# A sliding-window attention stage with its scores moved to the head of the turn

## The chip, the cores and the metric

One core of one Trainium2 chip runs the whole program. The metric is device time in microseconds (us); the kernel before takes 1373.77 us, the median of 3 runs (1372.44 to 1374.89). TensorE is PE in the profile (its weight loads are PEld), VectorE is DVE, ScalarE is ACT, GpSimd is POOL and SyncE is SP.

## The reference

A trunk of two layers on x (1024 tokens, width 1024, float32). Layer 0 normalises x, projects it once into six parts and runs two mixers side by side: a recurrent one (RG-LRU) and the sliding-window attention, whose stage the change rewrites. Layer 1 is a gated MLP with chunked spatial mixing; the change does not touch it. Cut to what matters:

```
z = rms_norm(x) @ w_in_a            # columns: za, ga (recurrent) | zq, zk, zv, gb (attention)
q = rms_norm(zq per head); k = rms_norm(zk per head)     # 16 query heads, 2 key/value heads, width 64
for each block of 128 queries:      # keys: the block before and the block itself, 256
    sc  = q @ k.T / 8 + bias[head]  # relative-position bias, -inf outside the window of 128
    m   = max(max(sc), sink[head])
    p   = exp(sc - m);  denom = sum(p) + exp(sink - m)
    out = (p / denom) @ v
y = concat(ya * silu(ga), yb * silu(gb));  x = x + y @ w_out_a
```

## The kernel before

**Precision.** Products run on pairs of float32r tiles, a high part and the rest (`hi` and `lo`, `h` and `l`), so one product is three matmuls (`mm3`, L144). Weights are split so by `load_weights` (L127): ScalarE casts the high part (L133), VectorE takes the rest (L134).

**Units.** The attention stage has 32 units: 4 groups `c` of 4 heads, times 8 blocks `b` of 128 tokens (`units`). A unit goes through these helpers:

- `att_bias` (L512): bias tile times the query's rms into `e`, two heads by GpSimd (L524) and two by ScalarE (L521). `e` has three buffers.
- `att_s` (L528): eight score matmuls into two PSUM banks, and per head one VectorE operation that scales, adds the bias and takes the maximum (L549); then `nm` (L554) and `es` (L557).
- `att_exp` (L560): exponentials on ScalarE, one for `es` and four for the heads, with sums.
- `att_scale` (L568): the two key blocks' probabilities are added (L573; because values are given as `v_more`, the difference of neighbouring blocks, one 128-wide product and a masked one do the work), then denominators, reciprocal and scaling.
- `att_pt` (L581): four transposes on TensorE, `ph` by ScalarE (L588), `pl` by VectorE (L589), and GpSimd's two masked copies `mh` and `ml` (L595).
- `att_pv` (L599): up to four matmuls into `pv`; ScalarE copies two halves to `ot` (L609, L610).
- `att_out` (L613): VectorE adds the other halves (L616, L617), GpSimd multiplies into `yb` (L619).

**The loop.** Turn t of the loop at L655 works on several units at once: scale of unit t-2, transposes and `pv` of t-3, bias and scores of t, exponentials of t-1. Between them TensorE gets filler work in halves of a projection, each 12 large matmuls: `q_step` makes the queries of the head group half a group ahead (two halves and then `q_parts`, which squares and splits the queries, and `q_stats`, eight small matmuls `st`, `qm` on VectorE, `pow` on GpSimd), `gb_step` the gate of the next group, and from group 3 on `mix_a_first` and `mix_a_part` the recurrent mixer's first products (`za`, `ga`). At the first unit of a group `gb_silu` (L360) takes ScalarE to the SiLU table over a 128x2048 tile.

**What sets the order.** `manual_schedule` keeps TensorE everywhere, and ScalarE, VectorE and GpSimd in this stage, in the order in which the code issues their instructions. In a turn of the kernel before VectorE's order is scale, `pl`, weight split, query remainders, `qm`, score operations, `es`, `out`; ScalarE's is `ph`, bias, exponentials, SiLU, weight cast, queries, evacuation of `gb`, `ot` copies; GpSimd's is masks, bias, `pow`, `yb`. PE's is transposes, `q_step`, `gb_step`, `pv`, statistics, scores. SP (the DMA queue) is ordered by the planner. `SPLIT_STEPS` says at which block b which weights are split; five weight tiles are held. The planner may also place work of the next stage (splits of the recurrent mixer's weights) into the end of this one. Eight PSUM banks are shared by all accumulators.

Of the kernel before, what the change touches and what calls it, by code (L numbers as in the profile page):

```python
# [14 lines left out]
ALU = mybir.AluOpType  # L15
# [3 lines left out]
P = 128  # L19
# [9 lines left out]
SPLIT_STEPS = {2: 7, 3: 8, 4: 9, 6: 10}  # L29
# [32 lines left out]
def trunk_kernel(  # L62
# [4 lines left out]
    nc = tc.nc  # L67
# [3 lines left out]
    x, out = x[0], out[0]  # L71
# [8 lines left out]
    def bank(name):  # L80
        return ps.tile([P, 512], F32, tag="p", name=name)

    def big_tile(dt, name):
        return big.tile([P, 2048], dt, tag="m", name=name)
# [42 lines left out]
    def load_weights(i, prefetch=True):  # L127

        for j in range(len(wtiles), min(i, last_spec[0]) + 1):
            fetch_weights(j)  # L130
            hi = wpool.tile(list(raws[j].shape), F32R, tag="wh", name=f"wh{j}")
            lo = wpool.tile(list(raws[j].shape), F32R, tag="wl", name=f"wl{j}")
            nc.scalar.copy(out=hi, in_=raws[j])  # L133
            nc.vector.tensor_tensor(out=lo, in0=raws[j], in1=hi.bitcast(F32), op=ALU.subtract)  # L134
            wtiles.append((hi, lo))
            if prefetch:
                fetch_weights(j + 2)
# [211 lines left out]
    def gb_step(c, f, half, khalf):  # L349

        if yb[c] is None:
            yb[c] = big_tile(F32, f"yb{c}").rearrange("p (f s) -> p f s", f=2)
        if khalf == 0:
            gb_acc[0] = bank(f"gb{c}_{f}_{half}")
        acc = gb_acc[0]
        proj_stationary_w(acc, ("gb", 2 * c + f), hh, hl, half * 512, khalf * 4, khalf * 4 + 4)
        return (yb[c][:, f, half * 512:(half + 1) * 512], acc) if khalf == 1 else None

    def gb_silu(c):
        nc.scalar.activation(out=yb[c], in_=yb[c], func=AF.Silu)  # L360
# [95 lines left out]
    units = [(c, b) for c in range(4) for b in range(NT)]  # L456
    state = [dict() for _ in units]
# [13 lines left out]
    def q_step(hc, j):  # L471

        c, half = divmod(hc, 2)
        p, kh = divmod(j, 2)
        if kh == 0:
            q_state["acc"] = bank(f"pq{hc}_{p}")
        proj_stationary_w(q_state["acc"], ("q", c, p), hh, hl, half * 512, kh * 4, kh * 4 + 4)
        return kh == 1
# [20 lines left out]
    def q_stats(hc, p, sq):  # L499

        acc = bank(f"st{hc}_{p}")
        for b in range(4):
            nc.tensor.matmul(acc[:, 2 * b:2 * b + 2], lhsT=sq[:, b, :], rhs=pair_ones, start=True, stop=True)
        m = small.tile([P, 8], F32, tag="qm", name=f"qm{hc}_{p}", bufs=2)
        rs = small.tile([P, 8], F32, tag="qrs", name=f"qrs{hc}_{p}", bufs=5)
        rms = small.tile([P, 8], F32, tag="qrms", name=f"qrms{hc}_{p}", bufs=5)
        nc.vector.tensor_scalar(out=m, in0=acc[:, :8], scalar1=1.0 / HD, scalar2=EPS, op0=ALU.mult, op1=ALU.add)
        nc.gpsimd.tensor_tensor(out=rs, in0=m, in1=half_neg, op=ALU.pow)
        nc.gpsimd.tensor_tensor(out=rms, in0=m, in1=rs, op=ALU.mult)
        q_state[hc][1].append((rs, rms))  # L510

    def att_bias(u):  # L512

        c, b = units[u]
        k0 = 0 if b else P
        e = at.tile([P, 4, 256], F32, tag="e", name=f"e{u}", bufs=3)
        for hp in range(2):
            rms = q_state[2 * c + b // 4][1][hp][1]
            if hp:
                for j in range(2):  # L520
                    nc.scalar.mul(e[:, 2 + j, k0:256], bias_tile(2 * c + hp)[:, j, k0:256],  # L521
                                  rms[:, 2 * (b % 4) + j:2 * (b % 4) + j + 1])
                continue
            nc.gpsimd.tensor_tensor(out=e[:, 2 * hp:2 * hp + 2, k0:256], in0=bias_tile(2 * c + hp)[:, :, k0:256],  # L524
                                    in1=bc(rms[:, 2 * (b % 4):2 * (b % 4) + 2], 2, 256 - k0), op=ALU.mult)
        state[u]["e"], state[u]["k0"] = e, k0
# [33 lines left out]
    def att_exp(u):  # L560
        st = state[u]
        e = st["e"][:, :, st["k0"]:256]
        nc.scalar.activation(out=st["es"], in_=st["es"], func=AF.Exp)
        for h in range(4):
            nc.scalar.activation(out=e[:, h], in_=e[:, h], func=AF.Exp,  # L565
                                 bias=st["nm"][:, h:h + 1], accum_out=st["sums"][:, h:h + 1])

    def att_scale(u):  # L568
        st = state[u]
        e = st["e"]  # L570
        p = st["p"] = e[:, :, 0:P] if units[u][1] else e[:, :, P:256]
        if units[u][1]:
            nc.vector.tensor_tensor(out=p, in0=p, in1=e[:, :, P:256], op=ALU.add)  # L573
        den = small.tile([P, 4], F32, tag="den", name=f"den{u}")
        nc.vector.tensor_tensor(out=den, in0=st["sums"], in1=st["es"], op=ALU.add)
        nc.vector.reciprocal(out=den, in_=den)
        nc.vector.tensor_tensor(out=p, in0=p, in1=bc(den, 2, P), op=ALU.mult)
# [3 lines left out]
    def att_pt(u):  # L581
        st = state[u]
        pt = bank(f"ppt{u}")
        for h in range(4):
            nc.tensor.transpose(pt[:, h * P:(h + 1) * P], st["p"][:, h, :], ident)
        ptv = pt.rearrange("p (j i s) -> p i j s", j=2, i=2)
        ph, pl = [at.tile([P, 2, 2, P], F32R, tag=f"p{r}", name=f"p{r}{u}", bufs=1) for r in "hl"]
        nc.scalar.copy(out=ph, in_=ptv)  # L588
        nc.vector.tensor_tensor(out=pl, in0=ptv, in1=ph.bitcast(F32), op=ALU.subtract)  # L589
        st["parts"] = [part.rearrange("p i j s -> p (i j s)") for part in (ph, pl)]  # L590
        st["before"] = []
        if units[u][1]:
            for r, part in zip("hl", st["parts"]):
                m = at.tile([P, 512], F32R, tag=f"m{r}", name=f"m{r}{u}", bufs=1)
                nc.gpsimd.affine_select(out=m, in_=part.bitcast(F32), pattern=[[0, 4], [1, P]], compare_op=ALU.is_ge,  # L595
                                        fill=0.0, base=-P, channel_multiplier=1)
                st["before"].append(m)
# [27 lines left out]
    def mix_a_part(n, kind, half, khalf):  # L625

        if khalf == 0:
            mix_acc[n, kind, half] = bank(f"{kind}{n}_{half}")
        proj_stationary_w(mix_acc[n, kind, half], (kind, n), hh, hl, half * 512, khalf * 4, khalf * 4 + 4)
# [6 lines left out]
    def mix_a_first(b):  # L636

        if b == 0:
            za0[0] = big_tile(F32, "za0").rearrange("p (i s) -> p i s", i=2)
        i, half, kh = b // 4, (b // 2) % 2, b % 2  # L640
        mix_a_part(0, ("za", "ga")[i], half, kh)
        return (za0[0][:, i, half * 512:(half + 1) * 512], mix_acc[0, ("za", "ga")[i], half]) if kh else None

    NU = len(units)
# [4 lines left out]
    sq = q_parts(0, 0)  # L649
# [2 lines left out]
        q_step(0, j)  # L652
    q_stats(0, 0, sq)
    sq = q_parts(0, 1)
    for t in range(NU + 3):  # L655
        c, b = divmod(t, NT)
        new = t < NU
        hc, j = t // 4 + 1, t % 4
        q_done, evac = False, None
        if 2 <= t < NU + 2:  # L660
            att_scale(t - 2)
        if t >= 3:
            att_pt(t - 3)
        if new:
            if hc < 8:
                q_done = q_step(hc, j)
            else:
                mix_a_part(1, "za", j // 2, j % 2)
            if t == 0:
                q_stats(0, 1, sq)  # L670
            att_bias(t)
        if 1 <= t <= NU:
            att_exp(t - 1)
        if new and c and b == 0:
            gb_silu(c)
        if new:
            evac = gb_step(c + 1, b // 4, (b // 2) % 2, b % 2) if c < 3 else mix_a_first(b)
        else:
            for kh in range(2):
                mix_a_part(*((1, "ga", t - NU) if t < NU + 2 else (2, "za", 0)), kh)  # L680
        if new and b in SPLIT_STEPS:
            load_weights(SPLIT_STEPS[b] + 4 * c)
        sq = q_parts(hc, j // 2) if q_done else None
        if evac:
            nc.scalar.copy(out=evac[0], in_=evac[1])
        if t >= 3:
            att_pv(t - 3)
        if q_done:
            q_stats(hc, j // 2, sq)
        if new:  # L690
            att_s(t)
        if t >= 3:
            att_out(t - 3)
    manual.__exit__(None, None, None)
    p1.close()
    const_c = ctx.enter_context(tc.tile_pool(name="const_c", bufs=1))
# [227 lines left out]

    manual = tc.manual_schedule(engines={ET.Activation, ET.DVE})
    manual.__enter__()
    for kh in range(2):
        mix_a_part(2, "za", 1, kh)
    conv = mix_a_conv(0)
    split = mix_a_split(0, conv)  # L930
    ys = [mix_a_silu(0)]
# [507 lines left out]
```

## Time and profile before

| | |
|---|---|
| median of 3 runs | 1373.77 us (1372.44 to 1374.89) |
| profiled execution | 1376.04 us, span 1374.3 us, granted TensorE clock 0.994 of full speed |
| busy over the span | PE 1329.9 us (97%), PEld 1123.6 (82%), DVE 1000.4 (73%), ACT 691.9 (50%), POOL 229.7 (17%) |
| chain that ended last | PE 68%, DVE 18%, ACT 4%, DMA 4%, issue 3%, POOL 2% |
| DMA | 131.38 MB in 97170 packets, mean 96 GB/s |
| attention stage | scores from 85.9 to 366 us, last `pv` product started at 387.51 |

The busy time of an engine is summed over the profiled span; a busy TensorE includes overlapping matmuls, so what counts is the spacing of their starts. In a timeline row stand the start, the duration, the engine, the line, the operation, output<-inputs, the shape and the count; in brackets the idle time just before it and what ended it.

### The profile page before, as it was taken

To read this page: it belongs to the slowest core of one execution; us is meant where nothing else is said; L and a number is where in the kernel's file an instruction comes from. 1 tells how busy PE (TensorE), PEld (TensorE's weight loads), DVE (VectorE), ACT (ScalarE), POOL (GpSimd) and SP (SyncE) were. 2 spreads that over 40 slices of the span, in tenths; PEclk is the share of its full clock that TensorE was granted. 3 is DMA by queue.
4 is the path that set the end of the run, shared out by engine and by line. 5 is a ranking of instruction groups with operands and counts; after the bars stand their busy time and mean duration, and the time that the engine had idled before them with its cause. 6 is when DMAs were issued, how large, how long until landed. Compare 5 with 4: busy or idle time off the path is not lost.

```text
span 1374.3 us, 17785 instructions
## 1 busy us (share of the span) xinstructions
PE 1329.9 (97%) x6775; PEld 1123.6 (82%) x6775; DVE 1000.4 (73%) x1622; ACT 691.9 (50%) x1246; POOL 229.7 (17%) x212
## 2 busy tenths in 40 slices
PE   7999999999889999989999899999999999999998
PEld 6987877777767888878888899888888888888887
DVE  6568787888767878996987655566666556669974
ACT  5466767676558778433554332344344444343331
POOL 2344545544413323000000000000000000000000
PEclk9999999999999999999999999999999999999999
DMA  6111111111211102511423332413332333497131
GB/s 220 38 42 46 31 46 32 47 31 47 62 43 39 50 23 108 210 65 62 153 108 100 100 108 93 139 62 107 108 109 69 107 109 114 141 376 255 50 113 62
DMA packets 97170, 131.38 MB, mean 96 GB/s; under 512 B 4907, under 2 KB 68540, under 8 KB 95036
## 3 DMA queue, kind: packets, MB, share of 16 engines
q1 hardware_dynamic: 97084, 130.24, 28.3%
q8 instruction: 53, 0.87, 0.3%
q14 instruction: 33, 0.27, 0.1%
HBM read 105.03 MB, written 25.19 MB: 95 GB/s over the span
## 4 chain that ended last, share of the span: by engine, by line
PE 68%; DVE 18%; ACT 4%; DMA 4%; issue 3%; POOL 2%; SPq 0%; DVEq 0%; ACTq 0%; POOLq 0%
PE m L145 6%; PE m L147 6%; PE m L146 6%; PE u L145 4%; PE u L146 4%; PE u L147 4%; PE g L145 3%; PE g L146 3%; PE g L147 3%; DVE e L549 3%; PE v L145 3%; PE v L147 3%; PE v L146 3%; PE s L1320 2%; PE pv L605 2%
## 5 line engine op out<-in xcount | busy, mean ns | idle before, releaser
L145 PE MATMUL m<-wh_w,wa 128*128 128x512 f32 x432 | 169.4, 392 | 4.1 <-DVE x L844 4.1
L147 PE MATMUL m<-wh_w,wa 128*128 128x512 f32 x432 | 168.6, 390 | 0.0
L146 PE MATMUL m<-wl_w,wa 128*128 128x512 f32 x432 | 168.6, 390 | 0.0
L145 PEld LDWEIGHTS m<-wh_w,wa 128*128 128x128 f32 x432 | 81.5, 189 | 21.8 <-ACT wa L709 4.9
L147 PEld LDWEIGHTS m<-wh_w,wa 128*128 128x128 f32 x432 | 81.4, 188 | 17.2
L146 PEld LDWEIGHTS m<-wl_w,wa 128*128 128x128 f32 x432 | 81.5, 189 | 16.7
L549 DVE CUSTOM_DVE_ANT_0 e<-ps,e,sink_bc 128x256 f32<-128x256 f32 (+1 forms) x128 | 62.4, 525 | 32.7 <-PE ps L546 28.8
L716 ACT CAST wh_w<-b 128x1024 fp32r<-128x1024 f32 x36 | 37.7, 1048 | 75.6 <-DVE b L811 52.7
L134 DVE TENSOR_TENSOR wl<-raw,wh 128x1024 fp32r<-128x1024 f32 x38 | 51.3, 1357 | 17.4 <-ACT wh L133 17.2
L565 ACT ACTIVATE e<-e,nm 128x256 f32<-128x256 f32 (+1 forms) x128 | 61.4, 481 | 0.0
L844 DVE TENSOR_TENSOR x<-m,x 128x512 f32<-128x512 f32 x56 | 36.7, 686 | 29.6 <-PE m L147 29.5
L145 PE MATMUL pq<-hh,wh 128*128 128x512 f32 x128 | 52.7, 411 | 0.0
L619 POOL TENSOR_TENSOR yb<-ot,yb 128x256 f32<-128x256 f32 x32 | 37.1, 1159 | 90.1 <-DVE ot L617 90.1
L145 PE MATMUL ga<-hh,wh 128*128 128x512 f32 x128 | 50.4, 394 | 1.4 <-ACT r L906 1.4
L717 DVE TENSOR_TENSOR wl_w<-b,wh_w 128x1024 fp32r<-128x1024 f32 x36 | 46.2, 1284 | 7.0 <-ACT wh_w L716 6.8
L1292 ACT ACTIVATE sg<-sg 128x512 f32<-128x512 f32 x24 | 15.2, 632 | 70.8 <-DVE sg L1291 70.8
L147 PE MATMUL pq<-hh,wl 128*128 128x512 f32 x128 | 50.4, 394 | 0.0
L146 PE MATMUL pq<-hl,wh 128*128 128x512 f32 x128 | 50.4, 394 | 0.0
L145 PE MATMUL za<-hh,wh 128*128 128x512 f32 x128 | 50.3, 393 | 0.0
L145 PE MATMUL gb<-hh,wh 128*128 128x512 f32 x128 | 50.2, 392 | 0.0
L146 PE MATMUL ga<-hl,wh 128*128 128x512 f32 x128 | 50.1, 391 | 0.0
L147 PE MATMUL ga<-hh,wl 128*128 128x512 f32 x128 | 50.0, 391 | 0.0
(401 smaller groups left out, 4078.3 us busy)
## 6 DMA issues: line engine op xcount, KB each, us to landing
raw<-in_w_in_a_dram SPq DMA_DIRECT2D x34, 512.0 KB, 4.1
b<-in_w_out_a_dram SPq DMA_DIRECT2D x22, 512.0 KB, 3.4
b<-in_w_out_c_dram SPq DMA_DIRECT2D x22, 512.0 KB, 5.9
rawg<-in_w_in_c_dram SPq DMA_DIRECT2D x16, 512.0 KB, 4.0
rawu<-in_w_in_c_dram SPq DMA_DIRECT2D x16, 512.0 KB, 3.5
vg<-vdram SPq DMA_DIRECT2D x8, 1024.0 KB, 6.9
ydram<-ug SPq DMA_DIRECT2D x32, 256.0 KB, 2.4
yg<-ydram SPq DMA_DIRECT2D x8, 1024.0 KB, 8.8
```

The costliest lines, as they stand in the source:

```text
L134: nc.vector.tensor_tensor(out=lo, in0=raws[j], in1=hi.bitcast(F32), op=ALU.subtract)
L145: nc.tensor.matmul(acc, lhsT=lh, rhs=rh, start=first, stop=False, skip_group_check=shared)
L146: nc.tensor.matmul(acc, lhsT=lh, rhs=rl, start=False, stop=False, skip_group_check=shared)
L147: nc.tensor.matmul(acc, lhsT=ll, rhs=rh, start=False, stop=last, skip_group_check=shared)
L549: nc.vector.tensor_tensor_reduce(out=e[:, h, k0:256], in0=acc[:, j * 256:j * 256 + kw], in1=e[:, h, k0:256], scale=rs[:, 2 * (b % 4) + j:2 ...
L565: nc.scalar.activation(out=e[:, h], in_=e[:, h], func=AF.Exp, bias=st["nm"][:, h:h + 1], accum_out=st["sums"][:, h:h + 1])
L605: nc.tensor.matmul(acc, lhsT=v[:, b, c // 2].rearrange("p r d -> p (r d)"), rhs=part, start=n == 0, stop=n == len(terms) - 1)
L619: nc.gpsimd.tensor_tensor(out=y, in0=flip(ot.rearrange("p (j s) -> p j s", j=2)), in1=y, op=ALU.mult)
L716: nc.scalar.copy(out=hi, in_=src)
L717: nc.vector.tensor_tensor(out=lo, in0=src, in1=hi.bitcast(F32), op=ALU.subtract)
L844: nc.vector.tensor_tensor(out=dst, in0=accs[m], in1=dst, op=add)
L1320: nc.tensor.matmul(acc[:, i * P:(i + 1) * P], lhsT=vgs[g][:, half * 4 + i, d * P:(d + 1) * P], rhs=ws_t[:, g, :], start=True, stop=True)
```

## The change

The add of the two key blocks goes from VectorE (in `att_scale`) to GpSimd, in a helper of its own, `att_add`, issued right behind the exponentials of the same unit. In the loop the scores come directly behind the transposes, ahead of all projections; the exponentials belong to the same unit t; scale goes to unit t-1 and transposes, `pv` and `out` to unit t-2, so the loop has one turn fewer. Bias and queries are made one unit ahead: bias of unit 0 and the first query half stand before the loop. The recurrent mixer's filler products come from one list, `spare`, and of the first products of channel block 2 one half more is left for behind the loop.

```diff
+    def att_add(u):
+        e, st = state[u]["e"], state[u]
+        p = st["p"] = e[:, :, 0:P] if units[u][1] else e[:, :, P:256]
+        if units[u][1]:
+            nc.gpsimd.tensor_tensor(out=p, in0=p, in1=e[:, :, P:256], op=ALU.add)
+
     def att_scale(u):
         st = state[u]
-        e = st["e"]
-        p = st["p"] = e[:, :, 0:P] if units[u][1] else e[:, :, P:256]
-        if units[u][1]:
-            nc.vector.tensor_tensor(out=p, in0=p, in1=e[:, :, P:256], op=ALU.add)
+        p = st["p"]
...
     sq = q_parts(0, 1)
-    for t in range(NU + 3):
+    q_step(1, 0)
+    q_stats(0, 1, sq)
+    att_bias(0)
+
+    spare = [(1, "za", h, kh) for h in range(2) for kh in range(2)] + \
+        [(1, "ga", h, kh) for h in range(2) for kh in range(2)] + [(2, "za", 0, 0)]
+    for t in range(NU + 2):
         c, b = divmod(t, NT)
         new = t < NU
-        hc, j = t // 4 + 1, t % 4
+        hc, j = (t + 1) // 4 + 1, (t + 1) % 4
         q_done, evac = False, None
-        if 2 <= t < NU + 2:
-            att_scale(t - 2)
-        if t >= 3:
-            att_pt(t - 3)
+        if t >= 2:
+            att_pt(t - 2)
         if new:
-            if hc < 8:
-                q_done = q_step(hc, j)
-            else:
-                mix_a_part(1, "za", j // 2, j % 2)
-            if t == 0:
-                q_stats(0, 1, sq)
-            att_bias(t)
+            att_s(t)
+        if hc < 8:
+            q_done = q_step(hc, j)
+        else:
+            mix_a_part(*spare.pop(0))
         if 1 <= t <= NU:
-            att_exp(t - 1)
-        if new and c and b == 0:
-            gb_silu(c)
+            att_scale(t - 1)
+        if new and b in SPLIT_STEPS:
+            load_weights(SPLIT_STEPS[b] + 4 * c)
         if new:
+            att_exp(t)
+            if c and b == 0:
+                gb_silu(c)
             evac = gb_step(c + 1, b // 4, (b // 2) % 2, b % 2) if c < 3 else mix_a_first(b)
         else:
-            for kh in range(2):
-                mix_a_part(*((1, "ga", t - NU) if t < NU + 2 else (2, "za", 0)), kh)
-        if new and b in SPLIT_STEPS:
-            load_weights(SPLIT_STEPS[b] + 4 * c)
+            mix_a_part(*spare.pop(0))
+        if t + 1 < NU:
+            att_bias(t + 1)
+        if new:
+            att_add(t)
         sq = q_parts(hc, j // 2) if q_done else None
         if evac:
             nc.scalar.copy(out=evac[0], in_=evac[1])
-        if t >= 3:
-            att_pv(t - 3)
+        if t >= 2:
+            att_pv(t - 2)
         if q_done:
             q_stats(hc, j // 2, sq)
-        if new:
-            att_s(t)
-        if t >= 3:
-            att_out(t - 3)
+        if t >= 2:
+            att_out(t - 2)
...
-    for kh in range(2):
-        mix_a_part(2, "za", 1, kh)
+    for half, kh in ((0, 1), (1, 0), (1, 1)):
+        mix_a_part(2, "za", half, kh)
     conv = mix_a_conv(0)
```

## Rows read from the trace of the kernel before

**Rows 1.** Windows, eight units: us busy (count) of PE PEld DVE ACT POOL; PEclk.

```profile
149.07:221.03 71.96, 68.41 (x353) 55.37 (x352) 59.74 (x162) 50.47 (x135) 36.21 (x39) 1.00 0.13 37
```

**Rows 2.** Waits, attention stage (80 to 395): us in total, times, longest.

```profile
PEld pv L605 <- DVE pl L589: 17.4, 21, 2.4
PEld pv L605 <- POOL ml L595: 16.3, 21, 1.3
```

**Rows 3.** Timeline, PE: start us, us, operation; each unit's first projection product.

```profile
157.35 0.48 PE L145 MATMUL pq<-hh,wh 128*128 128x512 f32 x1
...
166.13 0.48 PE L145 MATMUL pq<-hh,wh 128*128 128x512 f32 x1
...
173.94 0.48 PE L145 MATMUL pq<-hh,wh 128*128 128x512 f32 x1
...
374.41 0.48 PE L145 MATMUL ga<-hh,wh 128*128 128x512 f32 x1
...
381.24 0.48 PE L145 MATMUL za<-hh,wh 128*128 128x512 f32 x1
```

**Rows 4.** Timeline, ACT: one bias; a unit from exponentials to `ot` copies.

```profile
158.16 0.91 ACT L521 ACTIVATE e<-bias,qrms 128x256 f32<-128x256 f32 x2
...
248.25 0.21 ACT L563 ACTIVATE es<-es 128x4 f32<-128x4 f32 x1 [0.64 <-DVE es L557]
...
250.34 1.03 ACT L133 CAST wh<-raw 128x1024 fp32r<-128x1024 f32 x1
251.27 0.58 ACT L491 ACTIVATE sq<-pq 128x512 f32<-128x512 f32 x1
...
252.94 0.59 ACT L685 COPY yb<-gb 128x512 f32<-128x512 f32 x1
253.55 0.37 ACT L609 COPY ot<-pv 64x256 f32<-64x256 f32 x1
```

**Rows 5.** Timeline, DVE: `pl` and weight split; query remainders to add.

```profile
207.76 0.69 DVE L589 TENSOR_TENSOR pl<-ppt,ph 128x512 fp32r<-128x512 f32 x1
208.36 1.22 DVE L134 TENSOR_TENSOR wl<-raw,wh 128x1024 fp32r<-128x1024 f32 x1
...
325.70 1.39 DVE L495 TENSOR_TENSOR qs<-pq,qs 64x512 fp32r<-64x512 f32 x2
327.12 0.17 DVE L507 TENSOR_SCALAR qm<-st 128x8 f32<-128x8 f32 x1
327.32 0.54 DVE L549 CUSTOM_DVE_ANT_0 e<-ps,e,sink_bc 128x256 f32<-128x256 f32 x1
...
329.78 0.41 DVE L616 TENSOR_TENSOR ot<-pv,ot 64x256 f32<-64x256 f32 x1
...
330.66 0.69 DVE L573 TENSOR_TENSOR e<-e 128x512 f32<-128x512 f32 x1
```

**Rows 6.** Timeline of ACT, the first unit's exponentials begin.

```profile
88.96 0.20 ACT L563 ACTIVATE es<-es 128x4 f32<-128x4 f32 x1 [0.49 <-DVE es L557]
```

**Rows 7.** Timeline of ACT, the SiLU pass of a head group.

```profile
153.45 1.28 ACT L360 ACT_TABLE_LOAD   x1
154.74 1.91 ACT L360 ACTIVATE yb<-yb 128x2048 f32<-128x2048 f32 x1
```

**Rows 8.** Timelines, POOL and DVE: bias beside `nm`; a unit's POOL work.

```profile
95.96 1.04 POOL L524 TENSOR_TENSOR e<-bias,qrms 128x512 f32<-128x512 f32 x1
...
96.39 0.63 DVE L554 TENSOR_SCALAR nm<-mx 128x2 f32<-128x2 f32 x1
...
327.36 1.64 POOL L508 TENSOR_TENSOR qrs<-qm,half_neg 128x8 f32<-128x8 f32 x1 [4.10 <-DVE qm L507]
...
330.71 1.24 POOL L619 TENSOR_TENSOR yb<-ot,yb 128x256 f32<-128x256 f32 x1 [1.43 <-DVE ot L617]
331.90 0.63 POOL L595 TENSOR_SCALAR_AFFINE_SELECT mh<-ph 128x512 fp32r<-128x512 f32 x1
```

**Rows 9.** The windows view behind two waits of TensorE (columns as in rows 1).

```profile
119.00:122.00 3.00, 3.00 (x15) 2.90 (x14) 1.92 (x8) 1.05 (x3) 0.56 (x1) 0.51 0.59 175
```

## The prediction

> **What bounds the kernel now.** I read the windows first, to see which engine is near full in the attention stage; then the waits of that stage; then the timelines, engine by engine, for the loop that sets the length of a unit. In eight units TensorE is busy 68.41 of 71.96 us, VectorE 59.74, ScalarE 50.47, GpSimd 36.21 [rows 1]; the next eight units hold the same counts in the same 71.96. So TensorE is nearly the bound, but not quite: it waits in `pv` for `pl` (17.4 us over the stage) and for the masked `ml` behind it (16.3) [rows 2]. The lengths of units show what that costs. A unit that waits for nothing takes 166.13 to 173.94 = 7.81 without statistics of queries and 157.35 to 166.13 = 8.78 with them [rows 3]; a pair is 16.59. The trace has 71.96 / 4 = 17.99 per pair, so 1.40 per pair are waits. The loop behind them: scores (PE), four score operations, `out`, add, denominators, scale, `pl` (all DVE), `ml` (POOL), last `pv` and the next scores. A transfer ends none of these waits.
>
> **What the change does to that loop.** Scores come ahead of the projections, so `ml` is wanted only after 12 + 12 large matmuls. The loop above is gone, the add (0.69, the row at 330.66) leaves VectorE, and if nothing else came up a pair would fall to 16.59. But a new loop closes. Before, the exponentials of a unit ran one turn behind its scores. Now ScalarE's order in one turn is: `ph` of unit t-2, exponentials of t, bias of t+1, queries, evacuation, the two `ot` copies of t-2; and VectorE's is: `pl` of t-2, score operations of t, scale of t-1, weight split, query remainders, `qm`, `out` of t-2. Exponentials of t wait for score operations of t; these stand behind `pl`, which stands behind the preceding `out`, which waits for the `ot` copies, which stand on ScalarE behind the exponentials of t-1. All of it is serial, once per turn. Both queues are written out by hand, so nothing slips past. I sum it from one start of the exponentials to the next.
>
> Steps in every turn: exponentials 248.25 to 250.34 = 2.09, bias 0.91 [rows 4]; `out` 329.78 to 330.66 = 0.88, `pl` 207.76 to 208.36 = 0.60, score operations 327.32 to 329.78 = 2.46 [rows 5]; hops between engines about 0.15 together (ScalarE and VectorE start some 0.04 after what they wait for). That is 7.09.
>
> - Odd turn: evacuation 252.94 to 253.55 = 0.61 and the `ot` copies, twice 0.37 = 0.75 [rows 4]: 7.09 + 1.36 = 8.45.
> - Even turn to 26 (queries finished): square and casts 251.27 to 252.94 = 1.67 [rows 4], then VectorE's two remainders 1.39 and `qm` 0.20 ahead of `out` [rows 5]; the copies lie beside these. 7.09 + 3.26 = 10.35.
> - Even turns 28 and 30: 7.09 + 0.75 = 7.84.
>
> A pair is 18.80, above the 16.59 that TensorE needs and 0.81 above the 17.99 of today. TensorE is then idle in even turns, ahead of the statistics matmuls, whose square stands behind exponentials and bias.
>
> Counted out: exponentials of unit 0 start at 88.96 [rows 6] and can hardly start sooner, since their bias and statistics are no earlier. Unit 0 has half the keys, so its exponentials are estimated at 1.8 in place of 2.09: 1.8 + 0.91 + 1.67 + 1.39 + 0.20 + 2.46 + 0.1 = 8.5; unit 1 has `ph`, no `out`: 2.09 + 0.91 + 0.61 + 0.6 + 0.60 + 2.46 + 0.1 = 7.4. Unit 2 starts at 104.9. Then 13 even turns (134.6) and 12 odd ones (101.4): 340.9. Three SiLU passes now stand on the loop: table load 1.28 + 1.91 [rows 7], 3.2 each, 9.6; the three short units that begin a head group give back some 0.8 each (0.3 of the exponentials, the rest of the scores; an estimate): 348.1. The way back to the exponentials' table falls into ScalarE's wait.
>
> Turn 27 has a step of its own. The spare list asks for the weights `za` 1 there, before the turn's regular loading, and its split stands on VectorE behind the score operations: it ends 0.60 + 2.46 + 1.22 = 4.3 after `pl` starts [rows 5]. Two half products (2.3 left of one, 2.7) and `pv` (0.9) follow on TensorE, so the `ot` copies begin some 10.5 after `pl` started, against 0.60 + 2.46 + 2.09 + 0.91 + 0.61 + 0.1 = 6.8 otherwise: about 4 more. 27: 12.5, then 7.84, 8.45, 7.84: unit 31 starts its exponentials at 384.7. Scale of unit 30 comes 1.7 later, then two closing turns of 381.24 - 374.41 = 6.83 [rows 3]: last `pv` ends at 400.1. Today it ends near 381.24 + 6.83 - 0.36 = 387.7. That is +12.4. One half product of `za` 2 (about 2.7, half of what a closing turn holds beside transposes and `pv`) moves behind the loop, +2.7; there it covers the next stage's first waits on ScalarE and VectorE, for which I take 2.5 back. Sum without collisions: +12.6.
>
> Costed at nothing: GpSimd's add. Nearest rows: 1.04 for the bias of the same shape on GpSimd [rows 8], 0.69 on VectorE. It starts when exponentials end and is wanted after the next score operations, about 6 us later in an odd turn (0.91 + 0.61 + 0.75 + 0.88 + 0.60 + 2.46); twice its price would be hidden. `bias` has three `e` buffers, and the freed one's last reader is the transpose that opens the turn. The bias tiles' DMA keeps a turn between last use and next; with that cover gone it would cost its landing, a few us, three times. SP's order of weight loads doesn't change.
>
> **Collisions of VectorE and GpSimd.** At 95.96 GpSimd makes a bias (1.04), and VectorE's `nm`, 0.17 elsewhere, takes 0.63, until that bias ends [rows 8]. Today GpSimd is mostly idle during score operations. After the change it runs `yb`, two masks and the next bias exactly there, behind `pow` after an even turn: 1.64 + 0.73 + 0.63 + 0.63 + 1.04 = 4.7 us from `qm` (0.73: `yb` undisturbed, estimated from the 1.24 at 330.71, half a microsecond of which is a wait for the add) [rows 8]. VectorE gets from `qm` to `es` in 0.20 + 0.88 + 0.60 + 2.4 = 4.1. So `nm` and `es` fall into GpSimd's work. Bounds: 0 (VectorE always first) and two `nm` of 0.46 plus one whole bias 1.04, 2.0 a turn, 60 us. By the layout `es` waits out most of a bias after even turns, 0.8, and one `nm` the end of a mask after odd turns, 0.2: 13 x 0.8 + 17 x 0.2 = 13.8.
>
> The one row shows `nm` against a bias, nothing else. The Trainium skill (SBUF — State Buffer, Who interferes with whom) goes further: an instruction of VectorE in a two-port mode, or with two SBUF inputs, and one of GpSimd that reads SBUF block each other whole, whoever starts first. By that rule `es` and the masks count too, as in the layout; by the row alone only `nm` under a bias would, about 6 in place of 13.8, and the time would be near 1391.
>
> 12.6 + 13.8 = 26. The profiled execution is 1376.0 (span 1374.3 and 1.7 around it), 2.3 over the median. Steps back to back on ScalarE overlap by some 0.1, so I take 24 rather than 26: 1376 + 24 = 1400, and 1398 against the median 1373.8.
>
> **The rivals.**
> 1. TensorE sets the pace. If VectorE and ScalarE overlapped as their busy shares allow (59.74 and 50.47 of 71.96 [rows 1]), pairs would take 16.59: 1.40 x 16 = 22 saved, perhaps 5 more at the stage's end, less 4 in turn 27: near 1351. It decides if an even turn stays under 8.8. Against it: the serial sum is 10.35 and each link is a queue order or a data dependence. Chance 0.11.
> 2. A draw: no collisions, and half of the even turn's query steps hidden (1.3 x 13 = 17 off 12.6): within 3 us, near 1371 to 1376. Chance 0.06.
> 3. TensorE's clock as well. Between 119 and 122 it was granted 0.51, the lower level (1.2 GHz), behind two waits in `pv` [rows 9]. The new loop leaves TensorE idle about 2 us in each even turn. 3 us at half pace lose 1.5; slack of a pair is 2.2, or 3.2 with collisions, so mostly hidden; if not, 13 x 1 to 1.5 more: near 1415. Chance 0.15.
> 4. GpSimd's add comes late and the scale waits for it, so that the add's move does not help VectorE at all: it would need 6 us of delay. Under 0.02, no time of its own.
>
> Forecast (new serial loop): 0.66, from 1382 to 1412. The range takes in rival 3 and the upper part of the collisions, and leaves out rival 1 and most of 2: 1376 to 1420. About 0.2% (2.7 us) is what a measurement tells from no change: faster 0.12, same 0.05, slower 0.83.
>
> **What would show it.** Waits of `pv` for `pl` and `ml` gone or small; in their place VectorE's `out` waiting for `ot` copies, its score operations following `pl` without a wait for `ps`, ScalarE's `es` waiting for VectorE's `es` some 4 us in every turn, and statistics matmuls waiting for `sq`. Turns of about 11.2 and 8.6 in alternation, VectorE at 70 to 75% of eight units, `nm` and `es` with some durations of 0.4 to 1.2. One wait of 4 to 5 us for `wl` at the first `za` 1 product. I am wrong if turns alternate between 8.8 and 7.8, or if TensorE's waits lie elsewhere (a PSUM bank, a DMA of the bias).

## The result and the profile after

The changed kernel takes 1395.7 us (median of 4 runs, 1393.99 to 1398.35), the kernel before beside it 1374.33. The ratio is 1.0157, 95% interval 1.0135 to 1.0179: slower by 1.6%. The forecast was 1398. The profiled execution took 1398.35 us, its span 1396.6, with TensorE at 0.98 of full speed (0.994 before).

Windows of eight units, with the columns of [rows 1]; the second row is a stretch in which TensorE was granted the lower clock (0.50):

```profile
178.83:260.55 81.72, 72.75 (x352) 61.19 (x351) 52.61 (x153) 50.12 (x136) 37.87 (x45) 0.92 0.12 33
...
229.90:236.70 6.80, 6.80 (x27) 6.22 (x27) 5.73 (x17) 2.12 (x5) 4.21 (x6) 0.50 0.37 110
```

Eight units take 81.72, and so do the next eight, where they took 71.96. VectorE is busy for less (59.74 before, 52.61 now), and still everything is longer. No engine is full, so what sets the length must be a chain through several. The waits of the stage name it (us in total, times, longest):

```profile
ACT es L563 <- DVE es L557: 104.2, 31, 5.2
...
DVE ot L620 <- ACT ot L614: 56.2, 18, 7.7
DVE qs L495 <- ACT qs L493: 47.0, 15, 6.3
...
PE st L503 <- ACT sq L491: 30.7, 14, 3.5
```

The waits of `pv` for `pl` and `ml` [rows 2] are gone. ScalarE waits for VectorE in all 31 turns, 3.4 each on average, and VectorE waits back for ScalarE in `ot` or in `qs`. One even turn and the odd one behind it, first on ScalarE (the four exponentials and their sums left out):

```profile
206.67 0.20 ACT L563 ACTIVATE es<-es 128x4 f32<-128x4 f32 x1 [2.70 <-DVE es L557]
...
208.75 0.89 ACT L521 ACTIVATE e<-bias,qrms 128x256 f32<-128x256 f32 x2
209.55 0.57 ACT L491 ACTIVATE sq<-pq 128x512 f32<-128x512 f32 x1
210.03 1.16 ACT L493 CAST qs<-pq 64x512 fp32r<-64x512 f32 x2
...
217.73 0.20 ACT L563 ACTIVATE es<-es 128x4 f32<-128x4 f32 x1 [5.17 <-DVE es L557]
...
226.20 0.20 ACT L563 ACTIVATE es<-es 128x4 f32<-128x4 f32 x1 [2.70 <-DVE es L557]
```

and what VectorE, then GpSimd, did in these two turns:

```profile
211.21 1.39 DVE L495 TENSOR_TENSOR qs<-pq,qs 64x512 fp32r<-64x512 f32 x2 [2.36 <-ACT qs L493]
212.63 0.17 DVE L507 TENSOR_SCALAR qm<-st 128x8 f32<-128x8 f32 x1
212.83 0.42 DVE L620 TENSOR_TENSOR ot<-pv,ot 64x256 f32<-64x256 f32 x1
213.26 0.43 DVE L621 TENSOR_TENSOR ot<-pv,ot 64x256 f32<-64x256 f32 x1
213.72 0.69 DVE L593 TENSOR_TENSOR pl<-ppt,ph 128x512 fp32r<-128x512 f32 x1
214.33 0.54 DVE L549 CUSTOM_DVE_ANT_0 e<-ps,e,sink_bc 128x256 f32<-128x256 f32 x1
...
216.73 0.97 DVE L557 TENSOR_TENSOR es<-sink_bc,nm 128x4 f32<-128x4 f32 x1
...
224.51 0.33 DVE L554 TENSOR_SCALAR nm<-mx 128x2 f32<-128x2 f32 x1
```

```profile
216.64 1.04 POOL L524 TENSOR_TENSOR e<-bias,qrms 128x512 f32<-128x512 f32 x1
219.98 1.28 POOL L573 TENSOR_TENSOR e<-e 128x512 f32<-128x512 f32 x1 [2.30 <-ACT e L565]
...
224.19 0.62 POOL L599 TENSOR_SCALAR_AFFINE_SELECT ml<-pl 128x512 fp32r<-128x512 f32 x1
```

The links stand end to end: ScalarE's exponentials to 208.75 and its bias, square and casts to 211.21, then VectorE's remainders, `qm`, `out` and `pl` to 214.33, its score operations, and `es`. That `es` takes 0.97 in place of 0.16: GpSimd's bias began 0.09 us before it, and `es` ends when the bias does (217.70 and 217.68). That turn is 217.73 - 206.67 = 11.06, the odd one behind it 8.47.

Where the 22 us arise, by points of the two traces (starts, us):

| | before | after | difference |
|---|---|---|---|
| exponentials of unit 0 | 88.96 | 88.75 | -0.2 |
| last `pv` | 387.51 | 415.87 | +28.4 |
| first gate product `gt` | 398.64 | 429.72 | +31.1 |
| first output product `m` | 542.86 | 569.17 | +26.3 |
| first product of layer 1 (`v`) | 704.41 | 727.04 | +22.6 |
| end of the span | 1374.33 | 1396.64 | +22.3 |

### The profile page after: what moved, and what is told of

It is laid out like the page before. It is cut to its first block, busy times and chain, and to the rows that moved or that the text cites. A ratio compares the mean times of both kernels' runs of the same rounds, so it can differ in the third digit from the quotient of the medians.

```text
span 1396.6 us, 17901 instructions
## 1 busy us (share of the span) xinstructions
PE 1337.7 (96%) x6775; PEld 1138.0 (81%) x6775; DVE 970.2 (69%) x1594; ACT 691.2 (49%) x1246; POOL 235.8 (17%) x240
## 4 chain that ended last, share of the span: by engine, by line
PE 67%; DVE 15%; ACT 11%; DMA 4%; issue 2%; SPq 0%; POOL 0%; DVEq 0%; ACTq 0%
PE m L145 6%; PE m L147 5%; PE m L146 5%; PE u L147 4%; PE u L146 4%; PE u L145 4%; PE g L145 3%; PE g L146 3%; PE g L147 3%; ACT e L565 3%; DVE e L549 3%; PE v L145 3%; PE v L147 3%; PE v L146 3%; PE s L1328 2%
## 5 line engine op out<-in xcount | busy, mean ns | idle before, releaser
L563 ACT ACTIVATE es<-es 128x4 f32<-128x4 f32 x32 | 6.6, 205 | 104.2 <-DVE es L557 104.2
L495 DVE TENSOR_TENSOR qs<-pq,qs 64x512 fp32r<-64x512 f32 x32 | 22.0, 689 | 47.2 <-ACT qs L493 47.0
L147 PE MATMUL za<-hh,wl 128*128 128x512 f32 x128 | 50.7, 396 | 4.1 <-DVE wl L134 4.1
L620 DVE TENSOR_TENSOR ot<-pv,ot 64x256 f32<-64x256 f32 x32 | 13.3, 417 | 58.9 <-ACT ot L614 58.5
L146 PE MATMUL pq<-hl,wh 128*128 128x512 f32 x128 | 53.2, 416 | 0.0
L146 PE MATMUL za<-hl,wh 128*128 128x512 f32 x128 | 50.6, 395 | 0.0
## 6 DMA issues: line engine op xcount, KB each, us to landing
ydram<-ug SPq DMA_DIRECT2D x32, 256.0 KB, 2.4
```

The lines of the kernel that those rows point to most:

```text
L146: nc.tensor.matmul(acc, lhsT=lh, rhs=rl, start=False, stop=False, skip_group_check=shared)
L147: nc.tensor.matmul(acc, lhsT=ll, rhs=rh, start=False, stop=last, skip_group_check=shared)
L495: nc.vector.tensor_tensor(out=qs[(1 - j) * HD:(2 - j) * HD, 2 * p + j], in0=block(j * HD), in1=qs[j * HD:(j + 1) * HD, 2 * p + j].bitcast( ...
L620: nc.vector.tensor_tensor(out=ot[0:HD, :], in0=acc[0:HD, 0:256], in1=ot[0:HD, :], op=ALU.add)
```

## The experiments

The theory was the serial loop. Rivals were that single steps on it make the loss (the queries, the weights of `za` 1, GpSimd's own work) while the order as such is sound, or that TensorE's clock does. Each experiment edits the changed kernel, unless it says otherwise; ratios are to the kernel before, measured beside it. In the turns' numbers, turn t runs from the exponentials' start of unit t to that of t + 1; where the exponentials run a turn later, that is turn t + 1 of the loop. "Last `pv`" is the start of the stage's last product, in the profiled run.

**exp_a_turn_later.** The order is opened: exponentials run a turn behind their scores again, with the add on GpSimd and the scores first as in the change. With that go a bias made in its own turn, masks behind it, and two more half products inside the stage.

```diff
-        if t >= 2:
-            att_pt(t - 2)
+        if 2 <= t < NU + 2:
+            att_scale(t - 2)
+        if t >= 3:
+            att_pt(t - 3)
         if new:
+            att_bias(t)
             att_s(t)
+        if t >= 3:
+            att_mask(t - 3)      # GpSimd's masks, taken out of att_pt
...
-            att_scale(t - 1)
+            att_exp(t - 1)
+            att_add(t - 1)
...                               # pv and out of t - 3; spare keeps two more halves
```

> Scores stay at the head of the turn, queries stay one unit ahead and the add stays on GpSimd, but the exponentials run one turn behind the scores again (scale two, transposes and products three behind), and the bias is made in its own turn; the masks stand behind the bias on GpSimd; two more filler products fill the extra turn. Theory: no chain from one turn's exponentials to the next through VectorE is left, TensorE sets the pace, pairs of 16.6 to 17.2: about 1350, from 1345 to 1360. Rival A (collisions) and the rival that the add on GpSimd slows VectorE: between 1380 and 1396, since both stay.

Measured: 1352.85 us, ratio 0.9848 (0.9828 to 0.9867); last `pv` at 369.20. Nearly all turns are 7.7 to 8.3, near the two lengths of a unit that waits for nothing [rows 3]; a SiLU turn is 10.42 and the next 6.5, so the pass adds less than 1 us. The turn from the exponentials of unit 26 is 15.78 (the loop's turn 27), with TensorE waiting for the `za` 1 weights. The edit takes 43 us off. A part of that is collisions: the 32 `es` take 5.20 us here as they did before, in place of 14.40, since no bias runs beside them, and taking that away by itself (bias_behind_add, below) is worth 7.5. The other 35 go with the opened order: exponentials in the scores' own turn are most of the loss.

**queries_a_turn_later.** The other way to shorten the loop: the square, casts and remainders of finished queries move to the next turn, right behind the scores.

```diff
             att_s(t)
+        if late_q:
+            q_stats(*late_q[0], q_parts(*late_q[0], late_q[1]))
+            late_q = None
...
-        sq = q_parts(hc, j // 2) if q_done else None
+        if q_done:
+            late_q = (hc, j // 2), q_state["acc"]
```

> The changed kernel, but the finished queries are squared, split and summed one turn later, directly behind the scores of that turn; all else as changed. Theory (serial loop ScalarE to VectorE): the 3.26 us that these steps add to the loop in even turns go, since ScalarE does them while it waits for the score operations and VectorE behind its scale; even turns fall from 11.07 to about 8.1, odd ones rise to about 8.9 (their matmuls now hold the statistics); 13 pairs save some 2.5 each, 33 us: about 1363, from 1358 to 1372. Rival A (collisions of VectorE and GpSimd are the loss): at most 5 us, 1390 or more. Rival B (TensorE's lower clock): little, 1388 to 1396.

Measured: 1384.74, ratio 1.0079 (1.0060 to 1.0098), a miss. Even turns did fall, from 11.07 to about 8.0, but the odd turns from 3 to 25 rose to between 9.8 and 12.6. In the waits of the stage:

```profile
PE st L503 <- ACT sq L491: 24.2, 14, 4.0
ACT e L521 <- POOL qrms L509: 16.5, 8, 4.2
ACT yb L700 <- PE gb L147: 16.2, 6, 3.8
```

The statistics matmuls now stand in TensorE's queue ahead of both projections and wait there for ScalarE's square; the projections come late, and in every other odd turn ScalarE's evacuation of `gb` waits for them, on the loop. In the odd turns between, where the next half group's bias is due, ScalarE's bias waits for `qrms`, which these queries feed.

**queries_later_stats_mid.** The same, with the statistics matmuls behind the first projection half.

```diff
+        if late_q:
+            sq = q_parts(*late_q[0], late_q[1])
         if hc < 8:
             q_done = q_step(hc, j)
...
+        if late_q:
+            q_stats(*late_q[0], sq)
+            late_q = None
```

> As the run with queries finished a turn later (1384.7 us; its even turns fell to 7.97, but its odd turns rose to 10.5 to 11.1, since the statistics matmuls stood on TensorE ahead of the projections and waited there for the square), but the statistics stand between the two projections. Theory (query steps in the ScalarE-VectorE loop are the largest part of the loss): the even turns stay near 8.0, the odd ones fall to about 8.9, 17 a pair; 1360 to 1370. Rival (the odd turns' length is a loop of its own or TensorE's lower clock): stays above 1378.

Measured: 1372.1 (10 runs), ratio 0.9975 (0.9961 to 0.9990); last `pv` at 387.09. 1360 to 1370 was expected, so it falls short. Odd turns are 8.99 as expected in turns 5, 13 and 21, but 10.55 in turns 3, 11 and 19 and 9.85 in 7, 15 and 23. ScalarE in turn 11 (183.21 to 193.76; exponentials left out):

```profile
187.23 0.91 ACT L521 ACTIVATE e<-bias,qrms 128x256 f32<-128x256 f32 x2 [1.84 <-POOL qrms L509]
```

The bias of the next half group waits 1.84 for statistics that the edit made late. So the query steps do cost some 2.3 us in each even turn: of the 3.1 from 11.07 to 8.0, 0.8 is a collision of `es` with GpSimd (see the next run), which is gone here too (5.23 us for all 32 `es`, 14.40 in the changed kernel). Taking both out brings the kernel to where it was before, hardly further: the loop is still closed (ScalarE's `es` waits for VectorE's in every turn), and its turns are longer than TensorE's 7.81 and 8.78.

**bias_behind_add.** Two calls swapped: GpSimd makes the next bias behind the add, after the exponentials, and not beside the score operations.

```diff
-        if t + 1 < NU:
-            att_bias(t + 1)
         if new:
             att_add(t)
+        if t + 1 < NU:
+            att_bias(t + 1)
```

> The changed kernel with one swap in GpSimd's order: the add of unit t stands ahead of the bias of t+1, so that a bias no longer runs beside the end of the score operations. Theory with collisions as worked out (0.8 in even turns, 0.2 in odd ones): es no longer waits, even turns fall from 11.07 to about 10.3, some 10 to 12 us less: 1384 to 1387. Rival (order alone, collisions are nothing): 1396, no change.

Measured: 1388.23, ratio 1.0105 (1.0083 to 1.0128), 1.2 over the expected range. Regular even turns are 10.27, odd ones 8.46; last `pv` at 406.49, 9.4 sooner. VectorE's `es` in the stage (ns: least, median, most), first in the changed kernel, then in this one (in the kernel before it is 161, 163, 166):

```profile
L557 DVE TENSOR_TENSOR es<-sink_bc,nm x32: 161/164/971, 88.6 to 401.0; 128x4 f32<-128x4 f32 x32
```

```profile
L557 DVE TENSOR_TENSOR es<-sink_bc,nm x32: 161/164/165, 88.1 to 391.4; 128x4 f32<-128x4 f32 x32
```

Nothing on VectorE was changed, yet its longest `es` fell from 0.97 to 0.165, all 32 together by 9.2 us, and the even turns lost 0.80: the collision of `es` is shown, in its size too.

**silu_in_gap.** The SiLU pass is issued ahead of that turn's exponentials, into ScalarE's wait.

```diff
         if new:
-            att_exp(t)
             if c and b == 0:
                 gb_silu(c)
+            att_exp(t)
```

> The changed kernel with the SiLU pass of a head group issued ahead of that turn's exponentials, in the time in which ScalarE waits for the score operations. Theory (serial loop through ScalarE and VectorE): the pass of 3.2 us falls into a wait of some 4 us, but the way back to the exponentials' table (1.28) then stands behind the scores, on the loop. Turns 8, 16 and 24 fall from 13.85 by some 1.9 to 3.2 each, 6 to 9 us over the stage: 1387 to 1391. Rival (TensorE's clock and its waits set these turns, not ScalarE's queue): no change, 1394 to 1397.

Measured: 1389.34, ratio 1.0104 (1.0085 to 1.0123). Turns 8, 16 and 24 are 10.62 in place of 13.85, and the turns ahead of them 9.1 to 9.3 in place of 9.8 to 9.9. The pass fits the wait; its way back does not. ScalarE's `es` follows the second table load at once, while VectorE's `es`, the last row, had ended 1.04 before it. So some 1.0 a group stays on the loop, as was expected.

```profile
159.07 1.28 ACT L360 ACT_TABLE_LOAD   x1
160.36 1.92 ACT L360 ACTIVATE yb<-yb 128x2048 f32<-128x2048 f32 x1
162.28 1.28 ACT L563 ACT_TABLE_LOAD   x1
163.58 0.20 ACT L563 ACTIVATE es<-es 128x4 f32<-128x4 f32 x1
```

```profile
162.38 0.16 DVE L557 TENSOR_TENSOR es<-sink_bc,nm 128x4 f32<-128x4 f32 x1
```

Last `pv` comes at 404.41, 11.5 sooner in the profiled runs; the medians are 6 apart.

**za1_weights_early.** The weights of `za` 1 are loaded and split a turn sooner.

```diff
             load_weights(SPLIT_STEPS[b] + 4 * c)
+        if t == 26:
+            load_weights(20)
```

> The changed kernel, but the weights za 1 are split in turn 26, a turn before the spare list asks for them. Theory: turn 27 falls from 14.07 to about 8.5, 4 to 6 us less: 1390 to 1392. Rival (turn 27 is long for another reason, the end of the query projections): no change, 1396.

Measured: 1392.69, ratio 1.0123 (1.0089 to 1.0158), 0.7 over the expected range. Turn 27 is 8.47 in place of 14.07; last `pv` comes 5.9 sooner, the medians are 3.0 apart.

**add_on_vector.** The add of the two blocks back on VectorE, all else as changed.

```diff
-            nc.gpsimd.tensor_tensor(out=p, in0=p, in1=e[:, :, P:256], op=ALU.add)
...
+            nc.vector.tensor_tensor(out=p, in0=p, in1=e[:, :, P:256], op=ALU.add)   # in att_scale
```

> The changed kernel with the add of the two blocks back on VectorE, ahead of the denominators. Theory: VectorE idles over 2 us between scale and the next out, the add's 0.69 fits in there and is no part of the loop: 1394 to 1397, no change. Rival (GpSimd's add is what slows the kernel): 1385 or less. Rival (moving it off VectorE did help): 1410 or more, 0.69 in each of 28 units.

Measured: 1401.57, ratio 1.0196 (1.0172 to 1.0220), a miss: 1394 to 1397 was expected. Regular turns are 11.07 and 8.46 as in the changed kernel, and last `pv` comes 1.0 later. The profiled run is 4.2 us longer, the medians 5.9. Of the 4.2, 2.1 arise after the first `g` product of layer 1, which the edit does not touch; this trace has a stretch of 3.4 us at the lower clock there (at 916.8) that the changed kernel's has not, some 1.7 by itself, but why was not tested. By the stage alone the add's move gains about 1 us in the changed kernel, since the add lies in VectorE's waits either way; the times of the whole program leave open whether it is more.

**before_add_on_gpsimd.** The counterpart: the kernel before with nothing but the add moved, to GpSimd and to right behind the exponentials.

```diff
             att_exp(t - 1)
+            att_add(t - 1)       # on GpSimd; no add in att_scale
```

> The kernel before with one part of the change alone: the add of the two blocks on GpSimd, directly behind the exponentials. Theory: in the old loop (scores, VectorE, masks on GpSimd, products) the add stood on VectorE, with 0.69 and some 0.55 that the denominators waited for GpSimd; both go, 0.6 to 0.9 in some 22 waiting turns: 1358 to 1366. Rival (GpSimd's add collides as much as it frees): 1370 to 1378.

Measured: 1357.44, ratio 0.9872 (0.9846 to 0.9899), a little better than expected; last `pv` at 370.02. Eight units take 67.11, and TensorE's wait in `pv` for `pl` fell from 17.4 to 6.6, for `ml` from 16.3 to 4.8:

```profile
162.74:229.85 67.11, 66.62 (x353) 56.10 (x352) 52.71 (x153) 50.46 (x135) 44.59 (x45) 1.00 0.14 40
```

```profile
PEld pv L608 <- DVE pl L592: 6.6, 10, 2.3
PEld pv L608 <- POOL ml L598: 4.8, 10, 1.3
```

More went than the add. VectorE's `den`, right behind it, first in the kernel before, then in this one:

```profile
L575 DVE TENSOR_TENSOR den<-sums,es x32: 155/696/709, 97.1 to 376.5; 128x4 f32<-128x4 f32 x32
```

```profile
L578 DVE TENSOR_TENSOR den<-sums,es x32: 155/164/165, 97.3 to 358.4; 128x4 f32<-128x4 f32 x32
```

In the kernel before, GpSimd's `yb` was issued beside the add, lasted until the add and itself were done (330.71 to 331.95 [rows 8]), and held `den` for 0.70 in place of 0.16. That collision went with the add: 0.69 + 0.53 less on VectorE's part of the chain in each unit with two key blocks. The gain is less than that, 14 to 21 us (the interval), because TensorE, busy for 66.62 of 67.11, now sets the pace. The change holds one good part, about 17 us, and one that costs more than that.

**exp_later_za1_early.** The exponentials a turn later, with the weights of `za` 1 split in the loop's turn 26, so that the wait left in turn 27 goes.

> The version with the exponentials a turn later (1352.9 us) and the weights za 1 split in turn 26. In that version TensorE waits 1.7 and 5.3 us there and works some 3 us at the lower clock behind it. Theory: turn 27 falls from 15.78 to about 8, 6 to 9 us less: 1344 to 1347. Rival (the wait moves on to the next weight): 1350 to 1353.

Measured: 1344.5, ratio 0.9785 (0.9758 to 0.9811), the fastest version here, 2.1% under the kernel before. Last `pv` at 359.70; no stretch of the lower clock in the stage. Eight units take 65.96 with TensorE near full:

```profile
156.70:222.66 65.96, 65.43 (x352) 55.81 (x351) 53.12 (x153) 49.82 (x136) 40.13 (x46) 1.00 0.14 40
```

**exp_later_add_vector.** That version with the add back on VectorE.

> The version with the exponentials a turn later and the weights of za 1 early, but with the add of the two key blocks on VectorE, ahead of the denominators. Theory A (once the serial loop is open TensorE sets the pace, and VectorE has some 13 us free in each 64): the add's 0.69 per unit disappears in VectorE's waits, turns stay at 7.7 to 8.3, 1344 to 1350. Theory B (what made the kernel before faster by 16 us when the add went to GpSimd holds here too, so VectorE's work is what counts): 27 adds of 0.69 lengthen the stage by 14 to 19 us, 1358 to 1364.

Measured: 1349.1, ratio 0.9814 (0.9794 to 0.9834): 4.6 us over the one before it, last `pv` at 363.33, 3.6 later (1.7 of it in turn 30). Eight units take 66.53, 0.57 more for 7 adds of 0.69. So the same move is worth some 17 us where VectorE stands on the chain that TensorE waits for, 4 to 5 where TensorE sets the pace, and, by the stage, about 1 where a loop through ScalarE does.

## Why the prediction was right

The mechanism held: no wait of `pv`, ScalarE's `es` waiting for VectorE's in every turn, `st` waiting for `sq`, lengths of 11.07 and 8.46 in alternation. Opening the loop took 43 us off, some 35 of them beyond the collisions. One sign failed: VectorE is busy for 64% of eight units (52.61 of 81.72), not 70 to 75%. A part of what is missing is the wait of `den` for GpSimd in the kernel before, 0.53 a unit, which is gone with the add. By terms, with the collisions put in (0.8 in an even turn, 0.2 in an odd one):

| step | predicted | measured |
|---|---|---|
| regular even turn | 11.15 | 11.07 |
| regular odd turn | 8.65 | 8.46 |
| turns 0 and 1 | 16.1 | 16.70 |
| turns 2 to 26, three SiLU passes among them | 256.0 | 256.2 |
| turn 27 | 12.7 | 14.07 |
| turns 28 to 30 | 24.7 | 25.91 |
| exponentials of unit 31 to last `pv` (forecast: to its end) | 15.4 | 14.25 |
| last `pv` against before | +26.2 | +28.4 |
| behind it | +0.2 | -6.1 |

- **Collisions**, 13.8 predicted. Over the stage the 32 `es` take 14.40 us against 5.22 before, the 64 `nm` 15.13 against 11.34: 13.0 together. The row of before showed `nm` under a bias alone [rows 8]; in the trace of after `es` waits out a bias that began first (216.64 to 217.68, `es` to 217.70), and `nm` a mask (0.33 at 224.51, where `ml` ends at 224.81). That is what the Trainium skill says (SBUF — State Buffer, Who interferes with whom): an instruction of VectorE in a two-port mode, or with two SBUF inputs, and one of GpSimd that reads SBUF block each other whole, whoever starts first. `es` has two such inputs; that `nm`, with one, is in a two-port mode no run shows by itself. By the row alone (about 6) the sum would have been 7 us too low. The trace of before held a second such row that the prediction did not read as one, the `den` of 0.70 shown above.
- **Turn 27** took 1.4 more than forecast, and the lower clock accounts for it. TensorE waited 4.1 for `wl` as foreseen, and then ran its products at that clock, 0.43 apart until 366.4, where at full speed they are 0.23 apart; over eight products that is 1.6 (an estimate):

```profile
362.79 0.79 PE L147 MATMUL za<-hh,wl 128*128 128x512 f32 x1 [4.10 <-DVE wl L134]
363.38 0.63 PE L145 MATMUL za<-hh,wh 128*128 128x512 f32 x1
363.81 0.63 PE L146 MATMUL za<-hl,wh 128*128 128x512 f32 x1
...
366.62 0.40 PE L147 MATMUL za<-hh,wl 128*128 128x512 f32 x1
366.85 0.39 PE L145 MATMUL za<-hh,wh 128*128 128x512 f32 x1
```

- **Rival 3, the clock,** came true as a mechanism and not as a price. Ten stretches of the stage, 51 us together, ran at 0.50, the lower level (1.2 GHz); before it was 6.8 us. But the loop leaves TensorE so much slack that most turns hide it: only turns 7, 15 and 23 are longer for it (9.8 to 9.9 in place of 8.46, with the evacuation waiting for `gb`) and turn 27, some 5.6 us in all, where the rival had 13 or more. add_on_vector supports this: in the turn ahead of its turns 7 and 15 a lower stretch lasts 3.4 us, where it lasts 6.8 in the changed kernel, and they are 8.25 and 8.30; with 6.8 ahead of turn 23 it is 9.87.

```profile
159.17 0.59 ACT L695 COPY yb<-gb 128x512 f32<-128x512 f32 x1 [1.24 <-PE gb L147]
```

- **SiLU** went nearly as summed: 13.85 for a SiLU turn, 2.8 over a regular even one, where 3.2 less 0.8 was taken.
- **Turn 30** is 9.46 in place of 8.04: two weight casts stand on ScalarE ahead of the last exponentials, and a split on VectorE between the score operations and `nm`, which is not where the loop issues one. The forecast had counted nothing of the next stage's work.

```profile
398.41 1.05 ACT L133 CAST wh<-raw 128x1024 fp32r<-128x1024 f32 x1 [1.90 <-DMA raw<-in_w_in_a_dram]
400.67 1.05 ACT L133 CAST wh<-raw 128x1024 fp32r<-128x1024 f32 x1 [1.20 <-PE ga L146]
```

```profile
399.65 1.21 DVE L134 TENSOR_TENSOR wl<-raw,wh 128x1024 fp32r<-128x1024 f32 x1
```

- **The step that was mis-sized most** lies behind the stage: +2.7 for the half product moved there and 2.5 back. The first is right (last `pv` to first `gt` grew by 2.7). What comes back, up to layer 1, is far more than 2.5. TensorE's waits between last `pv` and first `v`, before and then after:

```profile
PE m L145 <- DVE x L844: 3.7, 1, 3.7
PE ga L145 <- ACT r L906: 1.4, 1, 1.4
PE gt L145 <- ACT xh L875: 1.4, 1, 1.4
PE gt L146 <- DVE xl L876: 1.0, 2, 0.8
PE gt L145 <- ACT z L864: 0.9, 1, 0.9
```

```profile
PE m L145 <- DVE x L852: 1.5, 1, 1.5
PE gt L146 <- DVE xl L884: 1.3, 1, 1.3
PE gt L145 <- ACT r L914: 0.6, 1, 0.6
```

Their sum falls from 8.4 to 3.4, by 5.0. The kernel before also has a stretch of 3.4 us at the lower clock behind its wait in `gt` (at 412.6) and one behind its wait in `m` (590.1); the changed kernel has neither, another 1.7 each (half of 3.4). 2.7 - 5.0 - 3.4 = -5.7, and the traces differ by 22.6 - 28.4 = -5.8. This is read from the two traces, not tested; why the wait of `m` is shorter is open. The versions in which the spare list leaves one half product only behind the loop have 9.3 from last `pv` to `gt`, but then 146.6 to 148.5 to `m`, against 144.2 with two halves (before) and 139.4 with three (changed): a half product left behind the stage costs 1.8 to 2.7 and gives at least that back.

So the mechanism was right, but that the time came out only 2.3 us under the forecast is luck: errors cancelled. The stage cost 2.2 more than summed, the work behind it 6.3 less, and the 2 that were taken off for overlaps don't show in the stage.

**The rivals that fell.** TensorE did not set the pace (rival 1, 1351): it does that once the exponentials run a turn later, at 1352.85 and 1344.5, so the price of that rival was right and only its condition was missing. A draw (rival 2) needed half of the query steps hidden; the version that takes them out of the even turns came to that draw, 0.9975, and its `es` meet no collision either. The add never came late (rival 4): 1.3 us on GpSimd, wanted some 6 us after the exponentials.

## What to carry to other kernels

Moving one producer ahead doesn't only remove its wait: write down, for every engine with an order by hand, what now stands between two passes through the same instruction, and add it up over engines. If that serial sum is over the busiest engine's share per turn, the loop sets the pace, and no engine's busy share will show it; keeping a stage's producer and its consumer a turn apart opens it. And try the parts of a bundled change one by one: here the move of one add was worth some 17 us by itself, and the reordering on top of it cost more than twice as much (the 21 us of the result and these 17). The parts don't add up freely: the reordering alone, with the add left on VectorE, costs 27 (add_on_vector).

## What the runs showed that was not expected

A tiny instruction can carry a collision's whole price: `es` on 128x4 took 0.97 in place of 0.16 in ten turns, in the turn shown because GpSimd had begun 0.09 us sooner; the score operations of 128x256, which read PSUM, took 0.53 to 0.54 in the same stretch. It goes the other way as well: GpSimd's add, 1.26 to 1.30 elsewhere, took 2.15 once, beside two weight splits of VectorE:

```profile
393.13 2.35 DVE L134 TENSOR_TENSOR wl<-raw,wh 128x1024 fp32r<-128x1024 f32 x2
```

```profile
394.49 2.15 POOL L573 TENSOR_TENSOR e<-e 128x512 f32<-128x512 f32 x1 [2.69 <-ACT e L565]
```

And a low clock need not cost much: 51 us at half pace are at most some 25 us of TensorE's work lost (half of them), and by the turns above the kernel is some 5.6 longer for it.
